# Seven small SBUF tiles made wider, so that the large buffers start at multiples of 128 bytes

## The chip, the core and the metric

The kernel runs on one core of a Trainium2 chip. The metric is the device time of one execution in microseconds (us). The kernel before was timed three times: 1390.62, 1392.78 and 1394.64 us, median 1392.78 us. All data are 32-bit floats; weights are read from HBM.

## The reference

A two-layer diffusion backbone over 256 latent tokens that follow 256 context tokens, model width 1024. Each layer is a mixer and a gated feed-forward network (FFN), each behind an RMS norm that is scaled and shifted by vectors computed from a conditioning vector:

```
x = x + mod[2] * mixer(modulate(rmsnorm(x), mod[0], mod[1]))
x = x + mod[5] * swiglu(modulate(rmsnorm(x), mod[3], mod[4]))
```

The mixer of layer 0 is 16 heads of a bidirectional state-space scan beside 4 heads of bidirectional retention; that of layer 1 is a bidirectional mLSTM with 4 heads of width 512. Layer 1 writes latent tokens only, and a last RMS norm follows. Nearly all the arithmetic is in the products with the weights: 1024 x 6160 into mixer 0, 2048 x 1024 out of it, 1024 x 4096 and 2048 x 1024 for the mLSTM, and 3 x 1024 x 2816 for each FFN.

## The kernel before

Features lie on the 128 partitions and tokens along the free axis, so a tile of 512 tokens is 2048 bytes on each partition. To keep 32-bit accuracy every operand of a weight product is split in two, a rounded part H and a remainder L in the type float32r, and each product is formed as three matmuls (`mm3`, lines 407 to 409: H by H, then H by L, then L by H, accumulated in PSUM). 512 columns stream through TensorE where context and latent tokens are taken together (layer 0: tiles hH, hL, uH, uL, yH, yL), 256 where they are taken apart or only one kind is needed (hp in the mLSTM, hHL and uHL in the second FFN, yHL in the mLSTM's output product) and where weights stream instead of activations (`projB`, line 704).

Weights come through a stream (lines 345 to 376): SyncE issues a 512 KB load into one of three `wraw` tiles (L355), ScalarE casts it to `wH` (L367), VectorE (now and then GpSimd) subtracts to make `wL` (L368 by way of the helper `tt`, whose line is L227). Vectors for the modulation come the same way: 512 KB tiles `ada` (in the buffers `adaraw`), multiplied by the conditioning `cbc` and summed on VectorE into a scratch tile `junk` (L267, L291). The first three feature chunks of the modulation are formed on TensorE instead, from tiles `adaf` and the small tile `cfeat` (L302). `cfeat` holds the two conditioning vectors as [128, 8, 2]; ScalarE's queue loads it with one DMA (L522), and ScalarE passes it through silu (L523) before its first squares of the input (L450, L453). The convolutions read padded tiles `xp` (L677, L682). Order on SyncE's queue is written out by hand; the other engines run their own instructions in program order, with background steps of the mixers placed between weight products by hand-made lists.

Tiles lie in SBUF one behind the other, pool by pool, in the order of their first use, and each one's size on a partition is rounded up to 32 bytes. The first pool holds constants, the residual `xt`, `wraw`, 36 working tiles of 2048 bytes (`s2`: hH, hL, hp, hHL, uH, uHL, xn, conv, qT, pT, acc, sq and most others), `wH`, `wL` and `xp`. Behind it lies a pool of layer 0 (`cbc`, `cfeat`, `ridx`, `rope`, `lg`, 8 tiles `s4` of 4096 bytes that hold adaf, vt, erow, xtok, yssd and yret, then `adajunk` and `adaraw`), whose place a pool of layer 1 takes later. All starts therefore follow from the sizes:

| tile | bytes on a partition | start before | past a multiple of 128 | start after | past a multiple of 128 |
|---|---|---|---|---|---|
| rowp | 416 | 17984 | 64 | 17984 | 64 |
| cst | 2048 | 18400 | 96 | 18432 | 0 |
| xt | 16384 | 20448 | 96 | 20480 | 0 |
| wraw (3) | 4096 | 38432 | 32 | 38528 | 0 |
| s2 (36) | 2048 | 50720 | 32 | 50816 | 0 |
| wH, wL (4 each) | 4096 | 124512 | 96 | 124672 | 0 |
| xp0, xp1 | 2080 | 157280 | 96, 0 | 157440 | 0, 0 |
| cbc | 8192 | 161440 | 32 | 161792 | 0 |
| cfeat | 64 | 169632 | 32 | 169984 | 0 |
| ridx | 4096 | 169696 | 96 | 170112 | 0 |
| s4 (8): adaf, vt, yret | 4096 | 175872 | 0 | 176384 | 0 |
| adajunk, adaraw | 2048, 4096 | 209152, 212224 | 0 | 209664, 212736 | 0 |
| mLSTM values v8 (4) | 8192 | 192928 | 32 | 193280 | 0 |

So before the change most large buffers start 32 or 96 bytes past a multiple of 128, which is 32 past a multiple of 64, but the `s4` tiles, `adajunk` and `adaraw` start at a multiple of 128 already.

The lines that make the seven tiles:

```python
rowp = const([P, NROW], "rowp")
cfeat = const([P, KD, 2], "cfeat", scoped=True)
epsc = const([P, 1], "epsc")
r = sb.tile([P, 4], F32, tag="rstd", name=nm("rstd"), bufs=2)
lg = const([P, 8], "lg", scoped=True)
xp = [const([P, 2, 260], f"xp{i}") for i in range(2)]
```

Of the kernel before, what the change touches and what calls it, by code (L numbers as in the profile page):

```python
# [19 lines left out]
KD = 8  # L20
# [8 lines left out]
NAF = 3  # feature chunks of the first shift and scale that TensorE forms  # L29


# ---------------------------------------------------------------- host layout
def _mtile(w, cols, ks):
    """[K, N] -> [128, nk * ncols]: partition = k within a k-chunk."""
    return np.concatenate([w[k * P:(k + 1) * P, cols] for k in ks], axis=1)


def _cols(v):
    """[n * 128] -> [128, n]."""
    return np.ascontiguousarray(v.reshape(-1, P).T)  # L40


def host_pack(i):
# [58 lines left out]
    # block-diagonal weights in compact form, [p = 4 b + row, tile, matrix, column]; the whole block of k on each of its  # L102
    # four partitions, and the gate weights of a block's four features on each of them
# [19 lines left out]
    # tables that depend on shapes alone  # L123
# [17 lines left out]
    # mLSTM masks [query tile it, direction]: over 512 keys (ctx | lat)  # L141
    mm = np.zeros((P, 4, T), np.float32)
    lo = np.where(j >= n, 0.0, NEG)  # i >= key
    hi = np.where(j <= n, 0.0, NEG)  # i <= key
# [10 lines left out]
# parameter columns  # L155
# [11 lines left out]
class _Bg:  # L167
    """Background work, advanced a stage at a time between the blocks of the main stream."""
# [18 lines left out]
def tile_hybrid(ctx, tc, A, out, dbg=None):  # L187
# [9 lines left out]
    def nm(p):  # L197
        uid[0] += 1
        return f"{p}_{uid[0]}"
# [33 lines left out]
    # ------------------------------------------------------------ constants  # L233
    prm = const([P, NPRM], "prm")
    rowp = const([P, NROW], "rowp")
# [4 lines left out]
    cfeat = const([P, KD, 2], "cfeat", scoped=True)  # L240
# [7 lines left out]
    epsc = const([P, 1], "epsc")  # L248
# [4 lines left out]
    # ------------------------------------------------------------ modulation vectors  # L253
# [30 lines left out]
    def ada_split(k, ts, units):  # L284
        """shift and scale of one feature chunk on the other engines: so many of the four sums on VectorE"""
# [12 lines left out]
    def ada_rows(ts):  # L298
        """shift and scale of one feature chunk, both streams, as rows"""
        p = scps()  # L300
        for kk in range(KD):
            TE.matmul(p[0:2, 0:256], lhsT=cfeat[:, kk, :], rhs=ts[kk // 4][:, kk % 4, :], start=kk == 0,  # L302
                      stop=kk == KD - 1)
        row = s2("arow")
        S.copy(out=row[0:2, 0:256], in_=p[0:2, 0:256])
        return p, row
# [7 lines left out]
    def cbc_make(st):  # L314
        """silu of one conditioning vector on every partition"""
# [21 lines left out]
    def ada(n, upto=80):  # L337
        """adds n to what may be done; does it"""
        adaquota[0] = min(adaquota[0] + n, upto)
        while adadone[0] + 1 <= adaquota[0]:  # L340
            next(adagen, None)
            adadone[0] += 1

    # ------------------------------------------------------------ weight stream
# [58 lines left out]
    def mm3(o, pairs, first=True, last=True):  # L403
        """o += sum over pairs of (lhsT H, L), (rhs H, L): three exact partial products."""
# [6 lines left out]
    def wk(w, k, n=P, o=0):  # L411
        """k-chunk of a weight tile: columns [k * n + o : + 128]"""
# [5 lines left out]
    # ------------------------------------------------------------ norms  # L418
    def rstd_a(accs, t0, t1, scale, eps, on_s=False):
        """[128 feat, tok] sums of squares -> [tok, tile] (mean + eps)^-0.5"""  # L420
# [6 lines left out]
        r = sb.tile([P, 4], F32, tag="rstd", name=nm("rstd"), bufs=2)  # L427
# [7 lines left out]
    def rstd_b(r, n):  # L435
        """broadcast over partitions, tokens along the free axis (PSUM)"""
# [5 lines left out]
    class Acc:  # L442
        """sum over feature chunks of x^2; the last chunks join in the cross-partition product"""
# [18 lines left out]
    class Split:  # L462
        """a [feature, token] operand as high and low parts; packed: context and latent tokens in tiles of their own"""
# [17 lines left out]
    def h_a(k, rb, am, sl):  # L481
        """one k-chunk of the norm for the tokens of sl, scaled; rb: rstd broadcast of these tokens"""
# [8 lines left out]
    def h_b(hk, k, xn, sh, sl):  # L491
        """shifted and split"""
# [8 lines left out]
    def log1p_exp_neg_abs(o, x, shape, tag):  # L501
        """o = log(1 + exp(-|x|)) with full relative accuracy (2 atanh(e / (2 + e)))."""
# [13 lines left out]
    # ------------------------------------------------------------ layer 0: norm, h, first four tiles, dt  # L516
    ridx = const([P, 2, T], "ridx", scoped=True)
    rope = const([P, 2, 256], "rope", scoped=True)
    lg = const([P, 8], "lg", scoped=True)
# [146 lines left out]
    # ------------------------------------------------------------ layer 0 mixer  # L666
    xp = [const([P, 2, 260], f"xp{i}") for i in range(2)]
# [5 lines left out]
    def conv(psum, wname, bname, t):  # L673
        """5-tap depthwise convolution over each stream; returns (padded input, result before silu)."""
# [11 lines left out]
    mods = iter(  # modulation vectors at each slot  # L686
        "001010002001100010000031000000020001000020200001000000010000001200000100000000000000000000000000")

    # background steps at each slot of the main stream
# [36 lines left out]
    def to_feat(tiles, keys, scales):  # L726
        """token-layout chunks [128 tok, 256] x4 -> split feature-layout tiles."""
# [11 lines left out]
    def ssd_decay(g):  # L739
        """dt_j exp(cs_i - cs_j) over [key j, head, query i] within each chunk, both directions summed"""  # L740
# [33 lines left out]
    def ssd_scan(g, fs, zs):  # L774
# [22 lines left out]
        # chunk contributions to the states: step n handles chunk F[n] forward and B[n] backward  # L797
# [32 lines left out]
        # outputs of the context chunks, then of the latent chunks  # L830
# [37 lines left out]
    def ret_qk(ps):  # L868
        """queries and scaled keys, latent tokens rotated"""
# [38 lines left out]
    def ret_decay(h):  # L908
        """decay of [key, query]: keys ctx0 ctx1 lat0 lat1 for latent queries (the last two serve context too)"""
# [14 lines left out]
    def ret_split(p, dm):  # L924
        """decayed products of two key tiles, as high and low parts"""
# [55 lines left out]
    def upd(m, p, gate, sl):  # L981
        """x += gate * p for the tokens of sl (p covers just these)"""
# [6 lines left out]
    class NormH:  # L989
        """norm of xt and modulation, a stage at a time"""  # L990
# [18 lines left out]
    def tail_tiles(ws, act, gate, acc, nrm, ms):  # L1009
        """the last output tiles of a phase: context tokens first, so that their norm runs under the latent ones"""  # L1010
# [18 lines left out]
    def head_tiles(nrm, n):  # L1029
        """the first n products of a phase, k outermost, context tokens first"""  # L1030
# [49 lines left out]
    # ------------------------------------------------------------ layer 1: block-diagonal weights, gate fold  # L1080
# [9 lines left out]
    def build_bd(t):  # L1090
        """block-diagonal weights of tile t, query-key form and values, and the values' gate weights"""
# [6 lines left out]
    def gate_fold():  # L1098
        """block-diagonal products folded: queries and keys into one form of the scores, all three into the gates"""
# [37 lines left out]
    # ------------------------------------------------------------ FFN  # L1137
# [50 lines left out]
    # ------------------------------------------------------------ layer 1: mLSTM  # L1188
# [68 lines left out]
    def gate_chain():  # L1257
        """gates in token layout [tok, tile, (dir: input gate 4, forget gate 4)] and their cumulative sums"""
# [28 lines left out]
        # sums of the chunks before: in place, then added  # L1287
# [139 lines left out]
    # P: a tile of the up projection through the convolution; A: its product ahead; Q, K: queries and values, scores;  # L1427
    # z: a tile of the gate; c: a step of the gates' chain; S: silu; h: a step of a head; d: two tiles of the down projection
# [26 lines left out]
    # ------------------------------------------------------------ layer 1 FFN (latent tokens)  # L1455
# [70 lines left out]
```

## Time and profile before

| | |
|---|---|
| time, median of 3 | 1392.78 us (1390.62 to 1394.64) |
| span of the profiled execution, first to last instruction | 1399.3 us |
| TensorE busy, matmul | 1324.7 us (95%), 8238 matmuls |
| TensorE busy, weight loads | 1169.2 us (84%) |
| VectorE, ScalarE, GpSimd busy | 1009.3, 655.0, 331.3 us |
| mean granted TensorE clock | 0.978 |
| DMA | 200.73 MB, 41.7% of 16 engines' span on SyncE's queue |

The profiled execution is one execution by itself: the span is its own time as the hardware profiler recorded it, 6.5 us above the median of the runs, and no other figure for it is given. The views read below are the chain of waits (back from the last instruction, at each step to what released it), the groups of instructions by line, tile and shape, the durations of one line's instructions (least, median, most), the timeline of one engine (start in us, duration in us, what), and the busy time by stretches. The ends of matmuls in the trace are modelled, so for TensorE the distance from one start to the next is what counts. Matmuls of plain f32 operands (not float32r) stand in the trace as two matmuls each.

### The profile page before, as it was taken

Reading aid. Unit: us, or ns where it says so; the run is one execution under the profiler, and the core shown is the slowest. Engines: PE = TensorE matmul, PEld = TensorE weight load, DVE = VectorE, ACT = ScalarE, POOL = GpSimd, SP = SyncE. Lnnn points to the kernel's source line nnn. Section 1 sums busy time; section 2 is a strip of 40 time slices with the busy share of each in tenths; the row PEclk is TensorE's granted clock in tenths of the full one; section 3 lists DMA queues with packets and bytes.
Section 4 is the critical chain, followed back from the end, with each engine's and each line's share of the span. In section 5 each row is a group of like instructions: output and inputs, shape, how many; then the busy total and the mean of one; then the engine's idle time right before and its main releaser. Section 6 shows DMA issues by size and latency. Waiting matters only on the chain.

```text
span 1399.3 us, 21319 instructions
## 1 busy us (share of the span) xinstructions
PE 1324.7 (95%) x8238; PEld 1169.2 (84%) x8238; DVE 1009.3 (72%) x1652; ACT 655.0 (47%) x1136; POOL 331.3 (24%) x254
## 2 busy tenths in 40 slices
PE   6999989989999999999999999989998979999997
PEld 2698868878888888888888888889998869999997
DVE  7997898887886658898557634676676998565555
ACT  4456645764745434221222133465666554444443
POOL 2246253752235221000000220412112351000001
PEclk9999999999999999999999999999999999899999
DMA  9245362624332223666547622311123324355553
GB/s 357 91 148 168 118 183 90 192 72 152 121 105 68 77 105 128 216 208 232 195 166 242 240 96 105 121 61 61 61 76 136 106 90 152 123 191 195 183 187 118
DMA packets 60840, 200.73 MB, mean 143 GB/s; under 512 B 6842, under 2 KB 8378, under 8 KB 60738
## 3 DMA queue, kind: packets, MB, share of 16 engines
q1 hardware_dynamic: 60594, 199.36, 41.7%
q8 instruction: 65, 1.06, 0.3%
q14 instruction: 37, 0.30, 0.1%
q10 hardware_dynamic: 144, 0.01, 0.0%
HBM read 197.16 MB, written 1.13 MB: 142 GB/s over the span
## 4 chain that ended last, share of the span: by engine, by line
PE 60%; DVE 16%; issue 10%; POOL 5%; ACT 4%; DMA 2%; SPq 0%; POOLq 0%; DVEq 0%; ACTq 0%
PE mm L407 18%; PE mm L408 18%; PE mm L409 18%; DVE wL L227 3%; DVE conv L682 2%; DVE junk L267 2%; PE mm L1222 1%; POOL yssd L227 1%; DVE junk L291 1%; DMA urow<-scr 1%; ACT wH L367 1%; DVE earg L1330 1%; POOL wL L227 1%; ACT erow L752 1%; DVE earg L1327 1%
## 5 line engine op out<-in xcount | busy, mean ns | idle before, releaser
L367 ACT CAST wH<-wraw 128x1024 fp32r<-128x1024 f32 x248 | 258.7, 1047 | 392.1 <-PE mm L408 251.4
L227 DVE TENSOR_TENSOR wL<-wraw,wH 128x1024 fp32r<-128x1024 f32 x230 | 296.8, 1292 | 128.1 <-ACT wH L367 120.5
L408 PE MATMUL mm<-hL,wH 128*128 128x512 f32 (+1 forms) x568 | 219.9, 388 | 1.3 <-DVE hL L498 1.3
L409 PE MATMUL mm<-hH,wL 128*128 128x512 f32 (+1 forms) x568 | 219.3, 387 | 1.3 <-DVE wL L227 1.3
L407 PE MATMUL mm<-hH,wH 128*128 128x512 f32 (+1 forms) x568 | 218.3, 388 | 1.4 <-ACT zs L770 1.4
L267 DVE SCALAR_TENSOR_TENSOR junk<-ada,cbc 128x1024 bf16<-128x1024 f32 x128 | 172.2, 1345 | 11.8 <-DMA ada<-in_ada 10.2
L409 PEld LDWEIGHTS mm<-hH,wL 128*128 128x128 f32 x568 | 107.4, 189 | 25.6 <-DVE wL L227 1.8
L408 PEld LDWEIGHTS mm<-hL,wH 128*128 128x128 f32 x568 | 107.3, 189 | 25.5 <-DVE hL L498 1.9
L407 PEld LDWEIGHTS mm<-hH,wH 128*128 128x128 f32 x568 | 106.7, 189 | 24.9 <-ACT zs L770 1.6
L682 DVE SCALAR_TENSOR_TENSOR conv<-xp,prm,conv 128x512 f32<-128x512 f32 x128 | 111.9, 879 | 17.3 <-ACT conv L679 16.1
L986 DVE SCALAR_TENSOR_TENSOR xt<-mm,mod,xt 128x256 f32<-128x256 f32 x144 | 64.6, 479 | 68.0 <-PE mm L409 67.9
L407 PE MATMUL mm<-wH,hH 128*128 128x256 f32 x384 | 111.0, 289 | 0.5 <-ACT conv L679 0.5
L408 PE MATMUL mm<-hp,wH 128*128 128x256 f32 x384 | 109.1, 285 | 1.1 <-DVE hp L498 1.1
L407 PE MATMUL mm<-hp,wH 128*128 128x256 f32 x384 | 109.0, 288 | 0.0
L409 PE MATMUL mm<-hp,wL 128*128 128x256 f32 x384 | 108.9, 285 | 0.0
L408 PE MATMUL mm<-wL,hH 128*128 128x256 f32 x384 | 108.2, 282 | 0.0
L409 PE MATMUL mm<-wH,hL 128*128 128x256 f32 x384 | 108.1, 282 | 0.0
L407 PE MATMUL mm<-hHL,wH 128*128 128x256 f32 x352 | 99.7, 285 | 1.1 <-ACT hHL L497 1.1
L408 PE MATMUL mm<-hHL,wH 128*128 128x256 f32 x352 | 99.9, 284 | 0.0
L409 PE MATMUL mm<-hHL,wL 128*128 128x256 f32 x352 | 99.8, 284 | 0.0
L227 POOL TENSOR_TENSOR acc<-acc,sq 128x256 f32<-128x256 f32 (+1 forms) x23 | 25.0, 1085 | 277.9 <-ACT sq L453 277.6
L407 PEld LDWEIGHTS mm<-hp,wH 128*128 128x128 f32 x384 | 74.3, 195 | 3.1 <-ACT conv L679 2.0
(345 smaller groups left out, 3256.3 us busy)
## 6 DMA issues: line engine op xcount, KB each, us to landing
wraw<-in_f SPq DMA_DIRECT2D x136, 512.0 KB, 3.3
ada<-in_ada SPq DMA_DIRECT2D x80, 512.0 KB, 4.5
wraw<-in_win SPq DMA_DIRECT2D x48, 512.0 KB, 4.2
wraw<-in_wup SPq DMA_DIRECT2D x32, 512.0 KB, 3.2
erow<-scr SPq DMA_DIRECT2D x16, 512.0 KB, 6.5
wraw<-in_wout SPq DMA_DIRECT2D x16, 512.0 KB, 3.8
wraw<-in_wdn SPq DMA_DIRECT2D x16, 512.0 KB, 3.3
adaf<-in_ada SPq DMA_DIRECT2D x10, 512.0 KB, 7.3
```

Source lines behind the costliest of these rows:

```text
L227: eng.tensor_tensor(out=o, in0=a, in1=b, op=op)
L267: V.scalar_tensor_tensor(out=junk, in0=raw, scalar=1.0, in1=cbc[:, st, :], op0=ALU.mult, op1=ALU.mult, accum_out=mod[l][c][:, k, st:st + 1])
L291: V.scalar_tensor_tensor(out=junk, in0=raw, scalar=1.0, in1=cbc[:, st, :], op0=ALU.mult, op1=ALU.mult, accum_out=to)
L367: S.copy(out=H, in_=raw)
L407: TE.matmul(o, lhsT=lh, rhs=rh, start=first and i == 0, stop=False)
L408: TE.matmul(o, lhsT=lh, rhs=rl, start=False, stop=False)
L409: TE.matmul(o, lhsT=ll, rhs=rh, start=False, stop=last and i == n - 1)
L682: V.scalar_tensor_tensor(out=o, in0=x[:, :, k:k + 256], scalar=pc(wname, t * 5 + k), in1=o, op0=ALU.mult, op1=ALU.add)
L752: S.activation(e[:, d, h], e[:, d, h], AF.Exp, bias=ncs[:, c, d, 4 * g + h:4 * g + h + 1])
L986: V.scalar_tensor_tensor(out=xt[:, m, half], in0=p[:, o:o + 256], scalar=gate[:, m, st:st + 1], in1=xt[:, m, half], op0=ALU.mult, op1=ALU.add)
L1222: TE.matmul(pv[:, c, :], lhsT=xm[:, c0 // 2, 2 + c * P:2 + (c + 1) * P], rhs=b[:, P:], start=True, stop=True)
L1327: V.tensor_tensor_reduce(out=e, in0=ur[d], in1=mmask[it * 2 + d], scale=-1.0, scalar=0.0, op0=ALU.add, op1=ALU.min, accum_out=negm[:, d:d ...
```

## The change

Seven tiles get more columns than they use, and the code keeps the used part of them. Both `xp` tiles have their two halves 272 instead of 260 columns apart, and `cfeat` has its pairs 4 instead of 2 columns apart, so that its one DMA writes eight pieces of 8 bytes on each partition instead of one piece of 64. Comments are also removed. Every other line is as before; the engines execute the same instructions in the same order on the same shapes, at other addresses.

```diff
-    rowp = const([P, NROW], "rowp")
+    rowp = const([P, 112], "rowp")[:, :NROW]
...
-    cfeat = const([P, KD, 2], "cfeat", scoped=True)
+    cfeat = const([P, KD, 4], "cfeat", scoped=True)[:, :, 0:2]
...
-    epsc = const([P, 1], "epsc")
+    epsc = const([P, 24], "epsc")[:, 0:1]
...
-        r = sb.tile([P, 4], F32, tag="rstd", name=nm("rstd"), bufs=2)
+        r = sb.tile([P, 16], F32, tag="rstd", name=nm("rstd"), bufs=2)
...
-    lg = const([P, 8], "lg", scoped=True)
+    lg = const([P, 32], "lg", scoped=True)[:, 0:8]
...
-    xp = [const([P, 2, 260], f"xp{i}") for i in range(2)]
+    xp = [const([P, 2, 272], f"xp{i}") for i in range(2)]
```

## Rows read from the trace of the kernel before

**Rows 1.** The page's chain of waits: share of the span by engine, then by engine and line.

```profile
PE 60%; DVE 16%; issue 10%; POOL 5%; ACT 4%; DMA 2%; SPq 0%; POOLq 0%; DVEq 0%; ACTq 0%
PE mm L407 18%; PE mm L408 18%; PE mm L409 18%; DVE wL L227 3%; DVE conv L682 2%; DVE junk L267 2%; PE mm L1222 1%; POOL yssd L227 1%; DVE junk L291 1%; DMA urow<-scr 1%; ACT wH L367 1%; DVE earg L1330 1%; POOL wL L227 1%; ACT erow L752 1%; DVE earg L1327 1%
```

**Rows 2.** Busy time by stretches of 100 us: stretch, its length, then busy us (and instructions) of TensorE matmul, TensorE weight load, VectorE, ScalarE and GpSimd, granted clock, busy share of the DMA engines, GB/s.

```profile
700.00:800.00 100.00, 100.00 (x430) 80.58 (x429) 62.54 (x93) 23.39 (x28) 3.16 (x3) 1.00 0.64 222
...
1200.00:1300.00 100.00, 100.00 (x832) 100.00 (x832) 58.81 (x80) 47.13 (x67) 0.00 (x0) 0.98 0.51 173
```

**Rows 3.** Timeline of TensorE's matmuls in three unbroken stretches, the first and the last of 25 matmuls in each (24 steps): start us, duration us.

```profile
700.01 0.40 PE L409 MATMUL mm<-hH,wL 128*128 128x512 f32 x1
...
705.61 0.40 PE L409 MATMUL mm<-hH,wL 128*128 128x512 f32 x1
...
1000.08 0.28 PE L407 MATMUL mm<-hp,wH 128*128 128x256 f32 x1
...
1002.80 0.28 PE L407 MATMUL mm<-hp,wH 128*128 128x256 f32 x1
...
1250.06 0.28 PE L409 MATMUL mm<-uHL,wL 128*128 128x256 f32 x1
...
1252.88 0.28 PE L409 MATMUL mm<-uHL,wL 128*128 128x256 f32 x1
```

**Rows 4.** Groups of TensorE instructions by line, tiles and shape: count, then busy us, mean ns of one, idle before. Lines 408 and 409 have groups of the same counts.

```profile
L407 PE MATMUL mm<-hH,wH 128*128 128x512 f32 x520 | 206.5, 399 | 1.4 <-ACT zs L770 1.4
L407 PE MATMUL mm<-wH,hH 128*128 128x256 f32 x384 | 111.0, 289 | 0.5 <-ACT conv L679 0.5
...
L407 PE MATMUL mm<-hp,wH 128*128 128x256 f32 x384 | 109.0, 288 | 0.0
...
L407 PE MATMUL mm<-hHL,wH 128*128 128x256 f32 x352 | 99.7, 285 | 1.1 <-ACT hHL L497 1.1
L407 PE MATMUL mm<-uH,wH 128*128 128x512 f32 x152 | 60.1, 396 | 0.0
...
L407 PE MATMUL mm<-uHL,wH 128*128 128x256 f32 x176 | 49.5, 281 | 0.0
...
L407 PE MATMUL mm<-yH,wH 128*128 128x512 f32 x112 | 45.7, 408 | 0.0
...
L407 PE MATMUL mm<-yHL,wH 128*128 128x256 f32 x128 | 35.9, 282 | 0.0
```

**Rows 5.** The durations of two lines' matmuls that stream 256 columns of plain f32, and of two lines' weight loads, all over the kernel: least, median and most ns, first and last start us. Under them the timeline's merged rows of one stretch of each line: start us, us from the first start to the last end, how many.

```profile
L302 PE MATMUL sc<-adaf,cfeat x48: 377/379/634, 18.2 to 47.2; 128*2 128x256 f32 x48
L943 PE MATMUL sc<-qT,qT x32: 377/379/483, 83.1 to 459.3; 128*128 128x256 f32 x32
L731 PEld LDWEIGHTS sc<-cst,yret x32: 138/141/146, 109.5 to 483.4; 128*128 128x128 f32 x32
L784 PEld LDWEIGHTS sc<-cst,conv x32: 138/141/143, 176.4 to 424.9; 128*128 128x128 f32 x32
...
28.25 3.61 PE L302 MATMUL sc<-adaf,cfeat 128*2 128x256 f32 x16
83.06 1.89 PE L943 MATMUL sc<-qT,qT 128*128 128x256 f32 x8
160.91 1.03 PE L731 MATMUL sc<-cst,yret 128*128 128x128 f32 x8
257.07 1.04 PE L784 MATMUL sc<-cst,conv 128*128 128x128 f32 x8
```

**Rows 6.** Timeline of float32r products of retention that stream vt (an `s4` tile) in lines 407 and 409 and vl (an `s2` tile) in line 408.

```profile
97.67 0.28 PE L407 MATMUL sc<-vt,pT 128*128 128x256 f32 x1
97.78 0.28 PE L408 MATMUL sc<-vl,pT 128*128 128x256 f32 x1
97.90 0.28 PE L409 MATMUL sc<-vt,pT 128*128 128x256 f32 x1
98.02 0.28 PE L407 MATMUL sc<-vt,pT 128*128 128x256 f32 x1
98.14 0.28 PE L408 MATMUL sc<-vl,pT 128*128 128x256 f32 x1
98.25 0.28 PE L409 MATMUL sc<-vt,pT 128*128 128x256 f32 x1
98.37 0.28 PE L407 MATMUL sc<-vt,pT 128*128 128x256 f32 x1
```

**Rows 7.** The durations of 1024-column instructions of ScalarE (L296, L367) and VectorE (L267, L227): least, median and most ns.

```profile
L296 ACT ACTIVATE ada<-ada x6: 1040/1046/1059, 24.2 to 57.5; 128x1024 f32<-128x1024 f32 x6
L367 ACT CAST wH<-wraw x248: 1027/1048/1103, 16.4 to 1381.4; 128x1024 fp32r<-128x1024 f32 x124
L267 DVE SCALAR_TENSOR_TENSOR junk<-ada,cbc x128: 1210/1224/3395, 81.4 to 787.7; 128x1024 bf16<-128x1024 f32 x128
L227 DVE TENSOR_TENSOR wL<-wraw,wH x230: 1162/1225/3399, 18.7 to 1382.5; 128x1024 fp32r<-128x1024 f32 x115
```

**Rows 8.** The page's list of DMA queues: packets, MB, the time of their packets as a share of 16 engines' span. q10 is ScalarE's queue, which has one DMA, that of `cfeat`.

```profile
q1 hardware_dynamic: 60594, 199.36, 41.7%
...
q10 hardware_dynamic: 144, 0.01, 0.0%
```

**Rows 9.** The start of ScalarE's timeline.

```profile
0.74 0.37 ACTq L522 DMA_DIRECT2D cfeat<-in_cfeat  x1
1.14 1.28 ACT L523 ACT_TABLE_LOAD   x1 [1.14 <-PEq L1514]
2.75 0.22 ACT L523 ACTIVATE cfeat<-cfeat 128x16 f32<-128x16 f32 x1 [0.33 <-DMA cfeat<-in_cfeat]
4.00 0.63 ACT L450 ACTIVATE acc<-xt 128x512 f32<-128x512 f32 x1 [1.03 <-DMA xt<-in_xt]
```

## The prediction, made before the changed kernel was run

> **What bounds the kernel now.** I read the chain of waits first, because a change of addresses counts only where it touches what ends last. TensorE holds 60% of the chain, and the three lines of the split products alone 54%; VectorE has 16%, ScalarE 4%, GpSimd 5%, waits for DMA 2% [rows 1]. The stretches say the same: in the FFNs (700 to 800 us and 1200 to 1300 us) TensorE is busy all the time, VectorE and ScalarE are below two thirds, and the DMA engines are at 0.64 and 0.51 [rows 2]. So the question is whether the start address of an operand sets the pace of a matmul, and only after that whether it sets the pace of the others.
>
> The pace of the products stands in the timeline. At 700 us 24 steps of 512 columns take 5.60 us, 233.3 ns each; at 1250 us 24 steps of 256 columns take 2.82 us, 117.5 ns each; at 1000 us 24 steps of the same shape take 2.72 us, 113.3 ns each [rows 3]. There are thus two paces of the 256-column product, 4.2 ns apart. Addresses don't tell them apart: at 1000 and at 1250 us all streaming operands (hp, uHL) start 32 past a multiple of 128 and all weights 96 past, by the table of starts.
>
> How many there are of each: of 512 columns 3 x (520 + 152 + 112) = 2352; of 256 columns 3 x (384 + 352 + 176) = 2736 with the tiles hH, hHL and uHL, which I count at the slower pace, and 3 x (384 + 128) = 1536 with hp and yHL, counted at the faster one [rows 4]. Their steps add up to 2352 x 233.3 + 2736 x 117.5 + 1536 x 113.3 ns = 548.7 + 321.5 + 174.0 = 1044 us, of which 54% of 1399.3 us, 756 us, lie on the chain: a share of 0.72. What is saved or lost on all of these steps therefore counts between 0.72 and 1 times.
>
> **The change part by part.** No instruction is added or taken away but the pieces of one DMA. The kernel before holds the comparison already, since the `s4` tiles and `adaraw` start at a multiple of 128 and the rest does not.
>
> *Plain f32 matmuls.* L302 streams 256 columns from adaf (start at 0), L943 from qT (32 past): median 379 ns for both. By steps, 16 matmuls from adaf take 3.61 us, (3.61 - 0.38) / 15 = 215.3 ns; 8 from qT take 1.89 us, (1.89 - 0.38) / 7 = 215.7 ns [rows 5]. Weight loads from yret (0) and from conv (32 past) both have the median 141 ns, and 8 of the transposes around them take 1.03 and 1.04 us [rows 5]. I cost these at 0; the bound from both sides is the 0.4 ns between the steps.
>
> *Float32r products, where the time is.* The nearest rows are retention's, where two of three matmuls stream from vt (0) and one from vl (32 past), with weights pT (32 past): six steps from 97.67 to 98.37 us take 0.70 us, 116.7 ns each [rows 6], beside 117.5 and 113.3 ns with no operand at a multiple of 128 [rows 3]. Two thirds of the streams aligned gain nothing that shows against the other pace, 0.8 ns against the slower. No row has both operands at 0, or 512 columns from 0. The lower bound is the 215.7 ns that plain f32 needs for 256 columns: taken as two slots a column, float32r without any loss would need 215.7 ns for 512 columns and 107.9 for 256. The upper bound is the slower pace everywhere. I take 0, since the row of vt is the same type, line and shape; both ends are priced as rivals.
>
> The Trainium skill, page "TensorE: Matmul & The Clock Gate", section "Wait — 56ns, not 53.3ns?", puts warm back-to-back matmuls at N / 2.4 GHz plus some 2.5 ns, 215.7 ns at 512 columns, measured there with bf16. Plain f32 keeps to that here at two slots a column, float32r with its 233.3 ns does not [rows 3, 5], so the page speaks for a loss that something other than columns causes, and a start address could be it; the sum by that would be the first rival's.
>
> *ScalarE and VectorE.* 1024 columns from 0 to 0 take ScalarE 1046 ns (L296), from 32 past to 96 past 1048 ns (L367). VectorE takes 1224 ns with one operand and the output at 0 (L267) and 1225 ns with all three off it (L227) [rows 7]. At 248 casts and 230 subtractions the 2 and 1 ns are worth 0.7 us, and most of that lies beside TensorE's work; I cost it at 0. The worst cases of VectorE, 3.4 us, occur in both groups, so addresses don't make them. The halves of `xp` lie 272 columns apart instead of 260: as many elements, other start addresses, and by the same rows nothing.
>
> *DMA into the moved buffers.* From 700 to 800 us loads of `ada` (0) and of `wraw` (32 past) are mixed, and the engines move 222 GB/s at a busy share of 0.64, 347 GB/s while busy; from 1200 us there is no `ada` any more (the last L267 starts at 787.7 us [rows 7]) and 173 / 0.51 = 339 [rows 2]. If all of the 2% were the address, it would shorten DMA waits, which are 2% of the chain [rows 1], 28 us, by under 1 us. I take 0; SyncE's queue keeps its order and its three `wraw` buffers. If the cover went, the next late thing would be the cast of the next weight tile.
>
> *The one DMA that changes.* `cfeat` is written in 1024 pieces of 8 bytes instead of 128 of 64. ScalarE's queue shows 144 packets at 0.0% of 16 engines' span [rows 8], so under 0.05% of 16 x 1399.3 us, 11.2 us, under 78 ns a packet. With 1040 packets that is between nearly 0 and 78 ns x 1040 / 16 = 5.1 us on each engine. Silu waits for it at 2.75 us, and behind silu in ScalarE's order the squares of the input wait for their own load until 4.00 us, idle for 1.03 us [rows 9]. So it costs between 0 and 4.1 us, at the head of a start-up in which everything follows those squares. I take 0, because a share that rounds to 0.0 is more likely far below its bound than at it.
>
> The sum is 0 with the ends -76 and +11 us. Against the profiled execution, 1399.3 us, it forecasts 1399.3 us; the runs shown lie 6.5 us lower, so the time is 1392.8 us. Runs of the kernel before spread by 0.3%, which is also about what a measurement of it can tell from no change.
>
> **The rivals.** *The loss of float32r is the address.* For it: 233.3 against 215.7 ns, with every weight and every 512-column stream off 128. Against it: the row of vt. If all starts at 128 took the loss away, it would save 2352 x 17.6 + 2736 x 9.6 + 1536 x 5.4 ns = 41.4 + 26.3 + 8.3 = 76 us, counted 0.72 to 1 times 55 to 76: about 1327 us.
>
> *Slow stretches take the faster pace.* Something that I can't name picks between 113.3 and 117.5 ns; other addresses may be enough to tip it. Then 2736 x 4.2 ns = 11.5 us, and if 512 columns went at twice the fast pace, 2352 x 6.7 = 15.8 us: 27.3 us, counted 20 to 27, 1366 to 1373 us, about 1370. Against it: the FFNs keep the slower pace without a break, and no operand of a product there moves by more than 64 bytes relative to the other.
>
> *Fast stretches take the slower pace* (the other side). Its place is the mLSTM from 870 to 1190 us; its price 1536 x 4.2 ns = 6.5 us, counted 4.7 to 6.5: 1397.5 to 1399.3, about 1399 us. It decides from some 1000 of the 1536 matmuls on, where 4.2 us is passed. For it: the pace there is the rarer one.
>
> *The pieces of cfeat hold up the start*: up to 4.1 us, 1397 us, just at the bound of what can be told; it decides only if a piece takes near 78 ns.
>
> That the change doesn't do what it says is ruled out by the table of starts, where every large buffer ends at 0.
>
> **How the numbers follow.** No effect 0.58, address loss 0.08, faster pace 0.14, slower pace 0.14, cfeat 0.06. The first alone would lie from 1389 to 1397. A range from 1366 to 1400 takes in the faster pace wholly, the slower one and cfeat, and leaves out the 0.08. Faster by over 0.3%: 0.08 + 0.14 and 0.03 of the first case, 0.25. Slower: 0.14, half of cfeat and 0.02 of the first, 0.19. Within: the rest, 0.56.
>
> **What would show it.** Right: L302 and L943 still at 379 ns, float32r steps at 113.3, 117.5 and 233.3 ns in the same stretches, L367 at 1048 and L227 at 1225 ns, some 1040 packets on ScalarE's queue, L450 starting near 4.0 us. The address rival shows as 512-column steps below 226 ns; the two of pace as steps that change between 113 and 118 ns in whole stretches; cfeat as L450 starting at 5 us or later. The prediction is wrong if a step, a cast or a subtraction has a new median, or if the time leaves 1389 to 1397 us with all of them as before.

## The result, and the profile after

The changed kernel takes 1406.42 us (median of 10 runs, 1403.14 to 1409.71) against 1394.76 us (median of 10, 1390.62 to 1403.57) for the kernel before on the same chip: a ratio of 1.0076, interval 1.0054 to 1.0097. It is slower by about 11.7 us, and outside the forecast range, whose top was 1400 us. (The ratios here and below are those on record with their 95% intervals; they are not the quotients of the two medians, and differ from them by up to 0.0026.) The profiled execution's span is 1407.9 us, 8.6 us more than that of the first profile; it took 1409.71 us and was the longest of the ten.

The page of the changed kernel, its busy times, ScalarE's queue and its chain of waits, answers to [rows 1, 8]:

```profile
PE 1338.9 (95%) x8238; PEld 1183.0 (84%) x8238; DVE 1009.4 (72%) x1652; ACT 654.9 (47%) x1136; POOL 332.0 (24%) x254
...
q10 hardware_dynamic: 1040, 0.01, 0.0%
...
PE 68%; DVE 14%; issue 8%; POOL 4%; ACT 3%; DMA 1%; POOLq 0%; SPq 0%; DVEq 0%; ACTq 0%
PE mm L407 20%; PE mm L408 20%; PE mm L409 20%; DVE wL L227 3%; DVE conv L682 2%; DVE junk L267 1%; PE mm L1222 1%; POOL yssd L227 1%; DVE earg L1330 1%; DMA urow<-scr 1%; DVE earg L1327 1%; POOL wL L227 1%; DVE comb L227 1%; ACT wH L367 1%; ACT erow L752 1%
```

VectorE, ScalarE and GpSimd are busy as long as before, within 0.8 us. TensorE is busy 14.2 us longer with the same 8238 matmuls, and the three lines of the split products go from 54% to 60% of the chain [rows 1]. So the time is sought in their pace. The timeline of TensorE in three unbroken stretches, first and last of 25 matmuls each (start us, duration us), answers to [rows 3]:

```profile
719.42 0.39 PE L407 MATMUL mm<-hH,wH 128*128 128x512 f32 x1
...
725.02 0.39 PE L407 MATMUL mm<-hH,wH 128*128 128x512 f32 x1
...
997.76 0.28 PE L408 MATMUL mm<-hp,wH 128*128 128x256 f32 x1
...
1000.60 0.28 PE L408 MATMUL mm<-hp,wH 128*128 128x256 f32 x1
...
1254.70 0.28 PE L408 MATMUL mm<-uHL,wH 128*128 128x256 f32 x1
...
1257.55 0.28 PE L408 MATMUL mm<-uHL,wH 128*128 128x256 f32 x1
```

512 columns take 5.60 us for 24 steps, 233.3 ns each, as before. The hp products take 2.84 us, 118.3 ns, where they had 113.3; uHL takes 2.85 us, 118.8 ns, where it had 117.5. Neither pace of before is left; both gave way to a third, slower one. The means over all products of these tiles, in the table further down, say it more clearly: 119.1 ns for hp and 118.7 ns for hHL and uHL.

What did not move: the medians (the middle one of the three ns figures) of plain f32 matmuls and weight loads, and of the 1024-column instructions of ScalarE and VectorE, answer to [rows 5, 7].

```profile
L302 PE MATMUL sc<-adaf,cfeat x48: 377/380/635, 17.3 to 47.8; 128*2 128x256 f32 x48
L943 PE MATMUL sc<-qT,qT x32: 377/379/484, 82.7 to 460.1; 128*128 128x256 f32 x32
L731 PEld LDWEIGHTS sc<-cst,yret x32: 138/141/143, 107.5 to 484.3; 128*128 128x128 f32 x32
L296 ACT ACTIVATE ada<-ada x6: 1042/1046/1060, 23.3 to 57.0; 128x1024 f32<-128x1024 f32 x6
L367 ACT CAST wH<-wraw x248: 1027/1048/1107, 15.6 to 1389.4; 128x1024 fp32r<-128x1024 f32 x124
L267 DVE SCALAR_TENSOR_TENSOR junk<-ada,cbc x128: 1207/1224/3431, 80.9 to 788.8; 128x1024 bf16<-128x1024 f32 x128
L227 DVE TENSOR_TENSOR wL<-wraw,wH x230: 1161/1225/3397, 17.8 to 1390.5; 128x1024 fp32r<-128x1024 f32 x115
```

The start of ScalarE's timeline, and the first product of the main stream on TensorE, answer to [rows 9]; the last line is that product in the first profile of the kernel before:

```profile
0.73 0.64 ACTq L522 DMA_DIRECT2D cfeat<-in_cfeat  x1
5.16 0.22 ACT L523 ACTIVATE cfeat<-cfeat 128x16 f32<-128x16 f32 x1 [2.47 <-DMA cfeat<-in_cfeat]
5.28 0.61 ACT L450 ACTIVATE acc<-xt 128x512 f32<-128x512 f32 x1
...
23.85 0.39 PE L407 MATMUL mm<-hH,wH 128*128 128x512 f32 x1
...
24.74 0.39 PE L407 MATMUL mm<-hH,wH 128*128 128x512 f32 x1
```

The DMA in 1040 packets lands late: silu starts at 5.16 us instead of 2.75, the first squares at 5.28 instead of 4.00. So the sign that the prediction named for the pieces of `cfeat`, L450 at 5 us or later, did come. But by the first wide product nothing of it is left: 23.85 us, and 24.74 us in the first profile of the kernel before.

### The profile page after: what moved, and what is told of

Read it like the earlier page. It is cut to its first block, busy times and chain, and to the rows that moved or that the text cites. A ratio compares the mean times of both kernels' runs of the same rounds, so it can differ in the third digit from the quotient of the medians.

```text
span 1407.9 us, 21319 instructions
## 1 busy us (share of the span) xinstructions
PE 1338.9 (95%) x8238; PEld 1183.0 (84%) x8238; DVE 1009.4 (72%) x1652; ACT 654.9 (47%) x1136; POOL 332.0 (24%) x254
## 3 DMA queue, kind: packets, MB, share of 16 engines
q10 hardware_dynamic: 1040, 0.01, 0.0%
## 4 chain that ended last, share of the span: by engine, by line
PE 68%; DVE 14%; issue 8%; POOL 4%; ACT 3%; DMA 1%; POOLq 0%; SPq 0%; DVEq 0%; ACTq 0%
PE mm L407 20%; PE mm L408 20%; PE mm L409 20%; DVE wL L227 3%; DVE conv L682 2%; DVE junk L267 1%; PE mm L1222 1%; POOL yssd L227 1%; DVE earg L1330 1%; DMA urow<-scr 1%; DVE earg L1327 1%; POOL wL L227 1%; DVE comb L227 1%; ACT wH L367 1%; ACT erow L752 1%
## 5 line engine op out<-in xcount | busy, mean ns | idle before, releaser
L367 ACT CAST wH<-wraw 128x1024 fp32r<-128x1024 f32 x248 | 259.0, 1048 | 399.2 <-PE mm L408 260.8
L227 DVE TENSOR_TENSOR wL<-wraw,wH 128x1024 fp32r<-128x1024 f32 x230 | 297.4, 1295 | 133.1 <-ACT wH L367 126.5
L267 DVE SCALAR_TENSOR_TENSOR junk<-ada,cbc 128x1024 bf16<-128x1024 f32 x128 | 175.4, 1370 | 12.7 <-DMA ada<-in_ada 11.2
L408 PE MATMUL mm<-hp,wH 128*128 128x256 f32 x384 | 111.3, 291 | 1.1 <-DVE hp L498 1.1
L407 PE MATMUL mm<-hp,wH 128*128 128x256 f32 x384 | 111.1, 293 | 0.0
L227 POOL TENSOR_TENSOR acc<-acc,sq 128x256 f32<-128x256 f32 (+1 forms) x23 | 25.0, 1085 | 279.5 <-ACT sq L453 279.2
```

The source lines that it names most:

```text
L227: eng.tensor_tensor(out=o, in0=a, in1=b, op=op)
L267: V.scalar_tensor_tensor(out=junk, in0=raw, scalar=1.0, in1=cbc[:, st, :], op0=ALU.mult, op1=ALU.mult, accum_out=mod[l][c][:, k, st:st + 1])
L367: S.copy(out=H, in_=raw)
L407: TE.matmul(o, lhsT=lh, rhs=rh, start=first and i == 0, stop=False)
L408: TE.matmul(o, lhsT=lh, rhs=rl, start=False, stop=False)
```

## The experiments

**Where to look.** One distance can be read from the table of starts. The activations' buffers (`s2`) are 2048 bytes apart and the halves of hp 1024; weight chunks are 512 apart. So one number describes every product of activations with weights: start of weights minus start of activations. Before it is 124512 - 50720 = 73792 = 288 x 256 + 64; after, 124672 - 50816 = 73856 = 288 x 256 + 128. Where the weights stream and the activations are loaded (`projB`) the sign turns: -64, which is 192, becomes 128. The change thus did two things at once: it moved the start of every large buffer to a multiple of 128, and the distance from 64 to 128. The first is the alignment theory, the second the spacing theory.

**One tile widened alone, one put back.**

```diff
 a1_rstd_only (the kernel before, with)
-        r = sb.tile([P, 4], F32, tag="rstd", name=nm("rstd"), bufs=2)
+        r = sb.tile([P, 16], F32, tag="rstd", name=nm("rstd"), bufs=2)
 a2_rstd_back (the changed kernel, with)
-        r = sb.tile([P, 16], F32, tag="rstd", name=nm("rstd"), bufs=2)
+        r = sb.tile([P, 4], F32, tag="rstd", name=nm("rstd"), bufs=2)
```

> The kernel before, with the reciprocal-root tile alone widened (4 to 16 columns). Activations (the 2048-byte buffers) still begin 32 past a multiple of 128, the weight buffers now also 32 past one: the distance from activations to weights goes from 64 to 128 past a multiple of 512, as in the changed kernel, while every start stays 32 past a multiple of 64. Spacing theory (the pace of float32r products follows the distance between the streamed buffer and the buffer from which weights are loaded): the slow, irregular pace of the changed kernel, hp and yHL products near 119 ns a step, ratio to before 1.006 to 1.009. Alignment theory (it follows where each buffer itself begins against 64 or 128 bytes): the kernel before's pace, hp near 114.5 ns, ratio 0.998 to 1.002. Other-tiles theory (cfeat, lg, the padded convolution input or the other constants did it): ratio 0.998 to 1.002.

> The changed kernel with the reciprocal-root tile alone put back to 4 columns. Activations begin at a multiple of 128, weights 64 past one: the distance is 64 again, as before the change, with every start at a multiple of 64. Spacing theory: the pace of the kernel before, hp and yHL near 114.5 ns, ratio to before 0.998 to 1.002. Alignment theory: the changed kernel's pace, hp near 119 ns, ratio 1.006 to 1.009. Other-tiles theory: ratio 1.006 to 1.009 as well.

The tile alone makes the kernel before slower: 1407.60 us against 1395.73, ratio 1.0059 (1.0035 to 1.0082), at the lower edge of what the spacing theory forecast. Put back, it takes the whole loss away from the changed kernel: 1396.92 us, 0.9993 (0.9972 to 1.0014), though its large buffers still start at multiples of 64 and the activations' at multiples of 128. The timeline of the hp products, 24 steps, first of the widened kernel, then of the one put back:

```profile
996.93 0.28 PE L408 MATMUL mm<-hp,wH 128*128 128x256 f32 x1
...
999.78 0.28 PE L408 MATMUL mm<-hp,wH 128*128 128x256 f32 x1
```

```profile
1001.53 0.28 PE L407 MATMUL mm<-hp,wH 128*128 128x256 f32 x1
...
1004.25 0.28 PE L407 MATMUL mm<-hp,wH 128*128 128x256 f32 x1
```

2.85 us at distance 128 with starts 32 past a multiple of 64 (118.8 ns a step), 2.72 us at distance 64 with starts at multiples of 64 (113.3 ns). The alignment theory falls: it forecast both the other way round.

**The other tiles.**

```diff
 a3_cfeat_xp_lg (the kernel before, with)
-    cfeat = const([P, KD, 2], "cfeat", scoped=True)
+    cfeat = const([P, KD, 4], "cfeat", scoped=True)[:, :, 0:2]
-    lg = const([P, 8], "lg", scoped=True)
+    lg = const([P, 32], "lg", scoped=True)[:, 0:8]
-    xp = [const([P, 2, 260], f"xp{i}") for i in range(2)]
+    xp = [const([P, 2, 272], f"xp{i}") for i in range(2)]
```

> The kernel before, with only cfeat, lg and the two padded convolution inputs widened; activations and weights lie where they lay before. Spacing theory and alignment theory: ratio 0.998 to 1.002, hp near 114.5 ns. Other-tiles theory: ratio 1.006 to 1.009.

1395.98 us, 0.9990 (0.9968 to 1.0011): no effect, although silu starts at 4.82 us here too.

**Other distances in the whole kernel.** The same tile at 24 and at 32 columns puts the distance at 192 and at 256.

```diff
 a4_rstd24, a5_rstd32 (the kernel before, with)
-        r = sb.tile([P, 4], F32, tag="rstd", name=nm("rstd"), bufs=2)
+        r = sb.tile([P, 24], F32, tag="rstd", name=nm("rstd"), bufs=2)
+        r = sb.tile([P, 32], F32, tag="rstd", name=nm("rstd"), bufs=2)
```

> The kernel before, with the reciprocal-root tile widened to 24 columns: activations 32 past a multiple of 128, weights 96 past one as before, but the distance from activations to weights is 192 past a multiple of 512 instead of 64. Spacing theory, if what counts is the distance modulo 128: the pace of before, ratio 0.998 to 1.002; if it counts modulo 256 or 512: hp steps anywhere from 113 to 119 ns, ratio 0.97 to 1.01. Alignment theory and other-tiles theory: the pace of before, ratio 0.998 to 1.002.

> The kernel before, with the reciprocal-root tile alone widened to 32 columns: the distance from activations to weights becomes a multiple of 256 for every product. Spacing theory, from the 16 distances measured alone (distance 0: 226.7 ns at 512 columns, 119.9 at 256): hH and uH steps fall from 233.3 to 227, some 2350 of them, -15 us; hp, yHL, hHL, uHL and wH,hH steps rise to near 120, some 4500 of them by 2 to 5 ns, +13 to +16 us; ratio 0.996 to 1.004, the stretch from 700 to 800 us faster than before and the stretch from 1200 to 1300 slower than before. Alignment theory: nothing changes anywhere, the two stretches take what they took before.

At 192: 1397.46 us, 1.0002 (0.9983 to 1.0020). The time is as before, but not the steps: 512 columns fall from 233.1 to 229.2 ns, streamed weights (now at 64 the other way round) from 117.7 to 114.6, hp rises to 117.0. A period of 128 would have left them alone. At 256: 1401.12 us, 1.0031 (1.0011 to 1.0051). Busy time by stretches of this kernel, as in [rows 2]:

```profile
700.00:800.00 100.00, 100.00 (x443) 82.81 (x442) 61.54 (x93) 24.16 (x28) 7.07 (x7) 1.00 0.66 228
1200.00:1300.00 100.00, 100.00 (x825) 100.00 (x825) 57.23 (x75) 45.86 (x65) 0.00 (x0) 0.99 0.53 174
```

In the wide stretch 443 matmuls instead of 430 fit into 100 us, in the narrow one 825 instead of 832: one distance serves one kind of product and harms the other.

**The distance by itself.** A kernel that holds nothing but float32r products in the order of `mm3`:

```diff
+    for name, off in (("hA", 0), ("hB", 32)):
+        t = at512(8 * 2048, off, name)
...
+    for j in range(16):
+        t = at512(4096, 32 * j, f"w{32 * j:03d}")
...
+    for h in hs:
+        for n in (256, 512):
+            for w in ws:
+                run(h, w, n)
```

`at512` makes a tile that begins so many bytes past a multiple of 512, and `run` issues 60 products.

> The whole model is left out; only float32r products remain, in the order of mm3 (H by H, then L by H with the same weights, then H by the other weights), 60 in a row on each of 16 weight buffers that begin 0, 32, ... 480 bytes past a multiple of 512, with 256 and then 512 streamed columns, first with activations at a multiple of 512 (hA), then with activations 32 bytes further (hB). No other engine works beside them except a one-column copy after each 12. Spacing theory: the step is a function of the distance from activations to weights alone, so that hB's row is hA's row moved by 32 bytes, within 1 ns; at 256 columns about 119 ns at distances 0 and 128, 113 to 118 at 64, 117 at 192, 114.6 at 320 and 117.6 at 448 (the last two from the products in which the roles are exchanged); at 512 columns about 233 at 64 and 128 and 227 to 231 at 192. Alignment theory: hA's row and hB's row differ by a like amount at every distance. If the period is 128 bytes, the row repeats four times over the 16 distances; if it is 512, it does not. Rival that the pace comes from what other engines do to the buffers meanwhile: one step, near 113 ns and 227 ns, at all distances.

Mean step in ns, start to start over 56 of the 60 products at each distance:

| distance, modulo 256 | 0 | 32 | 64 | 96 | 128 | 160 | 192 | 224 |
|---|---|---|---|---|---|---|---|---|
| 256 columns | 119.9 | 118.3 | 117.8 | 117.3 | 118.8 | 120.0 | 117.8 | 117.8 |
| 512 columns | 226.7 | 233.3 | 233.3 | 234.3 | 232.4 | 233.4 | 228.8 | 233.3 |

The upper eight distances and the rows of hB repeat these within 0.4 ns, but for one 116.7 at 480 (224 modulo 256), and but for the very first run, hA at 0 with 256 columns, which began with some 20 steps of 213 ns and is left out. So the step is a function of the distance, with a period of 256 bytes and not 128 or 512, wherever the two buffers themselves begin, and with every other engine but a small copy at rest. The 114.6 ns forecast for the distance 320 did not come: it has the 117.8 ns of 64. 512 columns at the distances 256 and 64 in the timeline, 24 steps each:

```profile
159.16 0.40 PE L263 MATMUL mm<-hA,w 128*128 128x512 f32 x1
...
164.76 0.40 PE L263 MATMUL mm<-hA,w 128*128 128x512 f32 x1
...
243.09 0.39 PE L264 MATMUL mm<-hA,w 128*128 128x512 f32 x1
...
248.53 0.39 PE L264 MATMUL mm<-hA,w 128*128 128x512 f32 x1
```

5.60 us at 64, 233.3 ns; 5.44 us at 256, 226.7 ns. But 113.3 ns, the faster pace of before, stands nowhere in the table. It was forecast as possible at 64, and something was missing.

**Several starts at one distance.** The same products in groups of 24, with one accumulator, so that each group waits for a copy of the one before it, the longer the larger r, its number at this distance:

```diff
+        p = psp.tile([P, 512], F32, tag="one", name=nm("one"), bufs=1)
...
+        S.copy(out=jk[:, 0:8 + 10 * r], in_=p[:, 0:8 + 10 * r])
```

> The whole model is left out: products of 256 columns (24 groups of 24 at each of eight distances, 0 to 224 bytes) and of 512 columns (8 groups each), each group waiting for a copy of the one before it out of the only accumulator, so that each starts after a stall of another length. What is asked is whether a distance has more than one pace, and whether the stall chooses it. Two-pace theory (at distance 64, 256-column products keep either 113.3 or 117.6 ns, whichever the start gave them): both values occur at distance 64, groups of each, and one value at the distances 0 and 128 (near 120 and 119). Rival, the faster pace comes from something else in the full kernel (what VectorE and ScalarE do meanwhile): 117.8 ns in all groups at 64, as when no stall stood between.

At distance 64, 21 of 24 groups settle at 113.3 ns within five steps and three stay at 117.8. At 192 it is the other way: 20 at 117.8, four at 113.3. At 0 all lie between 119.6 and 120.0 (the first, which began with steps of 213 ns, left out), at 128 between 118.4 and 119.1 but for two near 120. Two distances of which the forecast said nothing have two paces as well: at 224, 17 groups lie at 116.6 to 116.9 ns and seven at 117.6 to 117.9, which is where the single 116.7 of m1 belongs, and at 96, 12 at 117.1 to 117.4 and 12 at 118.4 to 118.9 (all over the last 17 steps). Groups of 512 columns lie within 1.7 ns of each other at every distance. Two groups at distance 64, second to last product, with the start of each:

```profile
186.56 0.38 PE L262 MATMUL one<-hA,w 128*128 128x256 f32 x1 [0.31 <-ACT jk L265]
186.78 0.28 PE L263 MATMUL one<-hA,w 128*128 128x256 f32 x1
...
189.27 0.28 PE L264 MATMUL one<-hA,w 128*128 128x256 f32 x1
...
220.14 0.39 PE L262 MATMUL one<-hA,w 128*128 128x256 f32 x1 [0.39 <-ACT jk L265]
220.37 0.28 PE L263 MATMUL one<-hA,w 128*128 128x256 f32 x1
...
222.96 0.28 PE L264 MATMUL one<-hA,w 128*128 128x256 f32 x1
```

22 steps from the second product to the last take 2.49 us in one (113.2 ns) and 2.59 us in the other (117.7 ns). Nothing differs but the start, after waits of 0.31 and 0.39 us.

**The kernel before, twice more.** No edit.

> The kernel before, unchanged, profiled once more. Two-pace theory (at distance 64 the 256-column products keep the pace that their start gave them, and the start differs between executions of one program): the hHL and uHL steps of the last stage lie either near 113.3 ns, and the run takes 1392 to 1397 us, or near 117.8 ns, as in the first profile, and it takes about 7 us more (1584 steps by 4.5 ns), 1401 to 1404. Rival, the program fixes the pace: 117.8 ns again, with whatever time.

> As b1_again, a further execution of the kernel before: hHL and uHL steps near 113.3 ns with 1392 to 1397 us, or near 117.8 ns with 1401 to 1404 us; of the two, and the first profile, not all alike if the start of the stretch decides.

One took 1404.03 us (span 1402.2), the other 1395.15 us (span 1393.3). The uHL products of the one and of the other, 24 steps:

```profile
1252.72 0.28 PE L409 MATMUL mm<-uHL,wL 128*128 128x256 f32 x1
...
1255.55 0.28 PE L409 MATMUL mm<-uHL,wL 128*128 128x256 f32 x1
```

```profile
1252.81 0.28 PE L408 MATMUL mm<-uHL,wH 128*128 128x256 f32 x1
...
1255.53 0.28 PE L408 MATMUL mm<-uHL,wH 128*128 128x256 f32 x1
```

2.83 us (117.9 ns) against 2.72 us (113.3 ns), in one program at the same addresses. Over the 1584 hHL and uHL products the means are 117.8 and 113.3 ns, 7.1 us, most of the 8.9 us between the two spans. The other runs of the kernel before, of which no traces are kept, fit this: of the 17 timed beside a5, v1 and v2, 12 took 1392.42 to 1395.69 us and five 1402.99 to 1406.70, none between.

**A version that uses it.** Weight tiles get a buffer each, 192 bytes wider, and each tile begins at the distance that suits its products.

```diff
+    def wtile(p, z):
+        n = wn[0]
+        want = 192 if n in rev else 64 if 62 <= n < 67 or n >= 128 else 0
+        i = 2 * (n % 4) + z
+        o = (want - 64 - 192 * i) % 256 // 4
+        t = sb.tile([P, 1072], F32R, tag=f"{p}{n % 4}", name=nm(p), bufs=1)
+        return t[:, o:o + 1024]
...
-        H = sb.tile([P, 1024], F32R, tag="wH", name=nm("wH"), bufs=4)
-        L = sb.tile([P, 1024], F32R, tag="wL", name=nm("wL"), bufs=4)
+        H, L = wtile("wH", 0), wtile("wL", 1)
+        wn[0] += 1
```

`wn` counts the weight tiles, z is 0 for H and 1 for L, and `rev` lists the tiles of `projB`. This is v1_three_distances; v2_wide_only has 64 instead of 192 there, and v0_all_64 has 64 for all.

> The kernel before, with each weight tile placed at the distance from the activations that its kind of product runs fastest at: 0 for products that stream 512 columns of activations, 64 for those that stream 256, and 192 for those that stream the weights (64 the other way round). If the pace of the products is what the time follows: 2350 steps at 512 columns fall from 233.3 to 227 ns (-15 us), the 1152 steps that stream weights fall from 117.7 to 113.5 to 117.7 (0 to -5 us), ratio 0.985 to 0.990. Rival: the products only wait longer for their weights, which ScalarE and VectorE prepare: steps as said, but a ratio of 0.994 to 1.000, with more idle time of TensorE before the products.

> As v1_three_distances, but only the products that stream 512 columns are moved, to distance 0; all others keep the distance 64 that they have in the kernel before. If the pace is what the time follows: ratio 0.987 to 0.992. Rival, the waits for weights eat it: 0.995 to 1.001.

> The weight tiles of v2_wide_only (a tile of its own for each of the eight buffers, each widened by 192 bytes), but with every product at the distance 64 of the kernel before. Distance theory: ratio 0.998 to 1.002, 512-column steps at 233.3 ns. Rival, that the separate tiles and not the distances made v2_wide_only faster: 0.990 to 0.995.

v1 takes 1386.53 us against 1394.85, ratio 0.9931 (0.9904 to 0.9958); v2 takes 1385.73 us, 0.9924 (0.9896 to 0.9951); v0, the same tiles without the distances, 1395.09 us against 1396.18, 0.9993 (0.9979 to 1.0008). Both v1 and v2 lie a little above their forecasts, 0.985 to 0.990 and 0.987 to 0.992, and cannot be told apart; v2 is about 9 us under the kernel before, where the changed one is 11.7 us over it. The busy times on v2's page, and 24 of its steps of 512 columns (L419 to L421 are the three lines of `mm3`):

```profile
PE 1309.9 (95%) x8238; PEld 1167.4 (84%) x8238; DVE 1006.5 (73%) x1652; ACT 655.0 (47%) x1136; POOL 336.0 (24%) x254
```

```profile
699.77 0.39 PE L419 MATMUL mm<-hH,wH 128*128 128x512 f32 x1
...
705.21 0.39 PE L419 MATMUL mm<-hH,wH 128*128 128x512 f32 x1
```

5.44 us, 226.7 ns. The third distance of v1 brings nothing that can be told: its streamed weights take 115.9 ns on average, in v2 116.7. TensorE is busy 1306.4 us in v1, 3.5 us less than in v2, but idle 78.2 us of the span (1384.6 - 1306.4), 4.2 us more; what it waits for there is not shown.

By the steps, 2352 x 6.0 ns = 14.1 us of v2 should have come from 512 columns; 9.1 us came between the medians. Where the rest went is not shown. Idle time of TensorE does not clearly hold it: 1383.9 - 1309.9 = 74.0 us in v2, and 74.6, 72.9 and 71.2 us in the three profiles of the kernel before. Part may lie in the granted clock, which stands at 2.4 or at 1.2 GHz: its mean is 0.973 of full speed in v2's profile and 0.978, 0.977 and 0.975 in those three. One less the mean, times the span, is 37.4 us withheld, against 30.8, 32.3 and 34.8 us; this is an estimate that takes TensorE as busy throughout.

## Why the prediction was wrong

Mean steps in ns, start to start, of the products with weights, in stretches of full granted clock (2.4 GHz) and without the steps that have a wait in them; then the sum over all products (counts by [rows 4], and 144, 144 and 96 small ones of hH, uH and yH, not shown) against the first profile, and the difference of the spans:

| kernel | distance | 512 columns | streamed weights | hp | hHL, uHL | yHL | sum of steps, us | span, us |
|---|---|---|---|---|---|---|---|---|
| before, first profile | 64 | 233.1 | 117.7 | 114.6 | 117.8 | 114.4 | 0 | 0 |
| before, b2_again | 64 | 233.1 | 117.7 | 115.8 | 113.3 | 114.5 | -5.6 | -6.0 |
| changed | 128 | 232.8 | 118.8 | 119.1 | 118.7 | 119.0 | +10.3 | +8.6 |
| a1_rstd_only | 128 | 232.4 | 118.8 | 118.7 | 118.7 | 119.0 | +8.8 | +5.4 |
| a2_rstd_back | 64 | 233.1 | 117.4 | 115.1 | 113.3 | 117.2 | -5.6 | -7.5 |
| a4_rstd24 | 192 | 229.2 | 114.6 | 117.0 | 117.8 | 117.8 | -8.1 | -3.3 |
| a5_rstd32 | 256 | 227.1 | 119.8 | 119.9 | 120.0 | 119.8 | +1.7 | +1.3 |
| v2_wide_only | 0 and 64 | 227.1 | 116.7 | 114.9 | 113.3 | 114.7 | -21.5 | -15.4 |

**The step that failed** is the second of the parts, float32r products at 0. "The kernel before holds the comparison already" asked whether an operand at a multiple of 128 is faster than one that is not. That was the wrong question: what counts is the distance between the operand that streams and the one that is loaded. The row of vt could not answer it, since its pairs lie at the distances 32 and 0, neither at the 64 that was left nor at the 128 that was reached. Nor was there a gain of 0.8 ns in it: six steps that read 0.70 us to two decimals are anything from 115.0 to 118.3 ns each. Put at nothing, the float32r steps at 128 add 10.3 us to the sum of the first profile, all of it at 256 columns.

**"Addresses don't tell them apart"** was true and misread. One distance has two paces, and the start of a stretch picks one (b1 and b2, and the groups of m2); from this it does not follow that another distance has the same two. **"The upper bound is the slower pace everywhere"** rested on that: 128 has a pace of its own, 119 ns, above both. The range's top came from this bound. Of the 13.6 us between the forecast 1392.8 and the measured 1406.42 us, 2.0 belong to the base, the median of three runs where that of ten is 1394.76 us.

**"No operand of a product there moves by more than 64 bytes relative to the other"** was held against a change of pace. The period is 256 bytes; 64 of them was the whole cause.

**The rivals.** That the fast stretches take the slower pace came nearest: hp and yHL did lose theirs, by 4.5 and 4.6 ns instead of 4.2 (7.0 us). The 2736 products that were counted at the slower pace lose 0.9 to 1.1 ns each (2.7 us), and the small ones make up most of the rest; 512 columns give 0.7 us back. The address rival, 512 columns below 226 ns, did not come from alignment, but 226.7 ns was to be had from the distance, and the trace of before shows it: retention has no such products, but the mLSTM's values (vH, vL with the weights pH, pL) lie at distance 0.

```profile
1090.21 0.39 PE L409 MATMUL sc<-vH,pL 128*128 128x512 f32 x1
...
1091.57 0.39 PE L409 MATMUL sc<-vH,pL 128*128 128x512 f32 x1
```

Six steps in 1.36 us, 226.7 ns, beside 233.3 for hH [rows 3]: the row that would have shown that float32r has more than one pace at 512 columns, too.

**What was right.** Plain f32 matmuls, weight loads, casts and subtractions at nothing: their medians are within 1 ns of before. The DMA's pieces within their bounds, and at nothing by the first wide product; a3, which carries them too, is no slower.

**What the runs do not bear out** is the share of the steps' sum that reaches the end, 0.72 to 1. It is 8.6 of 10.3 us for the changed kernel and 15.4 of 21.5 for v2, but 5.4 of 8.8 for a1 and 3.3 of 8.1 for a4, and a2 and b2 gain more than their sums. The span of one profile moves with other things too: b1 has hHL and uHL at the pace of the first profile and is still 2.9 us longer, v2 had less of the granted clock, and in a4 TensorE is idle for 1396.0 - 1317.1 = 78.9 us, 4.3 us more than in the first profile.

The first profile lay 6.5 us above the median of the three runs and had caught hHL and uHL at the slower pace, which between b1 and b2 is worth 7.1 us. Against an execution like b2 the profile of the changed kernel is 14.6 us longer, against one like the first profile 8.6, and the 11.7 us between the medians lie between.

## What to carry to other kernels

Where float32r products stand end to end, take the start of the loaded operand minus that of the streamed one, modulo 256, from the table of addresses before and after any change of a tile's size, however small: here 0 was best for 512 columns, 64 for 256, where most starts gave 113.3 ns, and 128 was good for neither. A padding that aligns every buffer sets all these distances at once and can lose what luck had given. And two executions of one kernel can differ by 7 us in 1395 in the pace of one stage alone, so look at the steps of each stage before a single profile is taken as the base.

## What was not expected of the hardware

The distance between two operands in SBUF, with no other engine at work but a small copy, moves a float32r product's step between 226.7 and 234.3 ns at 512 columns and, with the start, between 113.3 and 120.0 ns at 256. The Trainium skill, page "TensorE: Matmul & The Clock Gate", section "Step-by-step: what each phase is for", says that TensorE reads the streamed operand and the next weights through two independent ports, so that a load takes no read bandwidth from the running product. By that the distance should change nothing; the table of m1 says otherwise, and the measurement decides.

A run of 256-column products at the distance 64 or 192 has two paces, 113.3 and 117.8 ns, can keep one of them for a whole stage (hHL and uHL above), and gets it from its start: 21 of 24 starts at 64 gave the faster one, 4 of 24 at 192. At 96 and 224 there are two paces as well, closer together.

Left open: what the two reads share, whether the load itself slows the stream (every product here loads weights, and none without was tried), what in a start picks the pace, and which part of what the steps gain is lost before the end. Whether bf16 products have such distances was not tried either.
